# Modulation rows summed and turned by two picking matmuls per chunk, and the decay projection as fp32r products in the key stage

## The chip, the core and the metric

The kernel runs on one core of one Trainium2 chip. The metric is the device time of one execution in microseconds; the median of three runs before the change is 1827.17 us (1825.25 to 1828.84). Engines are named as in the profile: PE is TensorE, PEld its weight loads, DVE is VectorE, ACT is ScalarE, POOL is GpSimd, SP is the queue that issues most transfers. A line such as L281 is a line of the kernel before.

## The reference

One layer of a hybrid backbone on 256 latent tokens and 256 context tokens, 2048 wide. Both streams are first modulated by rows that come from a condition vector each, then projected by one matrix `w_in`:

```
sh_m, sc_m, ... = split(silu(c) @ w_ada + b_ada, 6)       # csh_m, csc_m from c_ctx
h_lat = x * (1 + sc_m) + sh_m;   h_ctx = ctx * (1 + csc_m) + csh_m
q, k, v, g, a_lr, p, bg = split(h @ w_in)                  # a_lr: 2 x 16 columns
z[d] = a_lr[:, 16d:16d+16] @ w_decay_up[d] + b_decay_up[d]  # d: forward, backward
log_decay[d] = log_sigmoid(z[d]) / 16
```

Keys, queries, values and decays go into a gated linear attention in both directions (4 heads, chunks of 64); latent scans start from the context's final state. A pooling branch runs beside it, both are gated, projected and normalised, and a SwiGLU network follows. All inputs are fp32.

## The kernel before

Weights arrive as 512 KB units of 128 x 1024 fp32 (`raw`) and are split into two fp32r parts, `hi` on ACT (L96) and `lo` on DVE (L97). A product is three matmuls on such parts (L155, L156, L158 where tokens are stationary; L125 and L129 where weights are). The modulated inputs are kept split in the same way, 16 slices of 128 channels, in the tiles `hl` (latent) and `hc` (context).

The first stage makes the inputs and the values `v` together, since modulation is needed slice by slice. `ada_chunk` makes the modulation of 1, 2 or 4 slices at a time: seven chunks, (0,1) (1,1) (2,2) (4,2) (6,2) (8,4) (12,4) as first slice and number n. For a chunk it

- sums `silu(cond) @ w_ada` in 16·n/4 units of 512 KB (`rw`, ten buffers); each unit is four plain fp32 matmuls with a 2-column stationary operand (c and c_ctx), one on each of four 32-column strips of the array, so that the sums lie in partitions 0-1, 32-33, 64-65, 96-97 of one PSUM bank (L281);
- copies or adds these strips into a row tile `rb` of 2 partitions, one operation per strip (L241, L243, L292);
- turns each 128 columns of the rows into a column, 2n small fp32 matmuls against a 2 x 2 identity (L295), and adds biases (L301);
- scales and shifts the input slices (`rx`, L307), adds their share of the decay projection `a_lr` to a PSUM bank `a_acc` by fp32 matmuls with a 32-column operand, one per slice and stream (L312), and splits them into `hl` and `hc`.

Four value blocks follow for every group of slices (L341 on); after each unit of value weights the generator `step` issues some of the next chunk's sums. Plain fp32 matmuls take two passes, so each counts as two instructions in the profile.

At the end of the values `a_acc` is copied, spread onto the partitions that the heads read by a selection table `selt` and a row of ones (L377, L378, two fp32 matmuls for each direction), and kept as `alr[d]`: parts hi, lo, hi of the rows at partitions 0, 32, 64, and bias rows. Then the PSUM pool of this stage is closed and one with four and four banks opened, and the key stage begins (`kT_half`, L125 and L129). `log_sigmoid` (L438) later multiplies `alr[d]` by `wd`, the decay weights of one head.

The order on each engine is made by a list scheduler that follows data, buffers and priorities; SP issues transfers in the order of that schedule and waits where a buffer is not free yet. A pool can wait for the whole pool whose place it takes, or tile by tile (`reuse_waits="tile"`).

## Time and profile before

| what | value |
|---|---|
| runs, median (lowest, highest) | 1827.17 us (1825.25, 1828.84) |
| profiled execution: time, span | 1823.62 us, 1821.7 us |
| granted clock, mean | 0.992 |
| busy: PE, DVE, ACT, POOL | 97%, 64%, 44%, 1% of the span |
| bytes read from HBM | 390.62 MB, 216 GB/s over the span |
| values stage | first matmul at 4.8 us, last value product at 261.3 us |
| key stage | first product at 267.15 us |
| head stage, first use of `alr` | 380.2 us |

A row of groups reads: line, engine, operation, output<-input by the program's names, shape, xcount | busy us, mean ns of one | idle time of the engine just before. A row of the timeline reads: start us, length us, engine, line, operation; x2 is two merged instructions, and brackets give an idle stretch before it with what ended it. Starts of matmuls are measured and their ends are modelled, so spacings of starts are the safer reading.

### The profile page before, as it was taken

What the parts mean: (1) busy time and instruction counts of PE and PEld (TensorE: products, weight loads), DVE (VectorE), ACT (ScalarE), POOL (GpSimd) and SP (SyncE); (2) the same over time, 40 slices, a digit from 0 to 9 for tenths busy, and PEclk for the clock granted to TensorE, in tenths of its full rate; (3) what the DMA queues carried; (4) which work ended last, traced back from release to release, by engine and by line L of the source; (5) the groups of instructions that cost most, each with busy time, mean ns of one, the idle gap of its engine ahead of it and who ended that gap; (6) DMA issues with size and microseconds to landing.
All of it is one profiled execution on the core that took longest, in us unless ns stands there. A gap on an engine that the chain in (4) does not pass through costs nothing.

```text
span 1821.7 us, 24845 instructions
## 1 busy us (share of the span) xinstructions
PE 1773.5 (97%) x9596; PEld 1466.1 (80%) x9596; DVE 1167.8 (64%) x1740; ACT 804.3 (44%) x1182; POOL 9.6 (1%) x20
## 2 busy tenths in 40 slices
PE   6999999999999999999999989999999999999996
PEld 3666778878777788888888878888888888888886
DVE  3555457578768888865656665678865556554555
ACT  2212222256666554454444454454444444433332
POOL 0000000000000000000000000000000000000000
PEclk9999999999999999999999989999999999999998
DMA  8696238576535688865557635579976555555553
GB/s 336 227 338 233 82 128 300 193 249 225 168 110 184 220 304 317 291 210 191 190 193 276 204 112 187 192 249 314 329 267 197 187 193 186 182 192 193 196 187 125
DMA packets 109702, 394.35 MB, mean 216 GB/s; under 512 B 12224, under 2 KB 12864, under 8 KB 109072
## 3 DMA queue, kind: packets, MB, share of 16 engines
q1 hardware_dynamic: 107712, 384.05, 61.6%
q0 software_dynamic: 1872, 8.72, 1.3%
q8 instruction: 75, 1.23, 0.3%
q14 instruction: 43, 0.35, 0.1%
HBM read 390.62 MB, written 2.10 MB: 216 GB/s over the span
## 4 chain that ended last, share of the span: by engine, by line
PE 64%; DMA 4%; DVE 3%; ACT 2%; issue 1%; SPq 0%; DVEq 0%; ACTq 0%
PE ps L125 28%; PE ps L129 14%; PE ps L158 6%; PE ps L155 6%; PE ps L156 6%; DMA raw<-in_w_o 1%; DMA ra<-in_w_adaT 1%; DVE lo L97 1%; ACT hi L96 1%; DMA raw<-in_w_fi 0%; DVE ra L267 0%; PE ps L110 0%; PE ps L494 0%; PE ps L112 0%; PE ps L111 0%
## 5 line engine op out<-in xcount | busy, mean ns | idle before, releaser
L97 DVE TENSOR_TENSOR lo<-raw,hi 128x1024 fp32r<-128x1024 f32 x510 | 622.2, 1222 | 415.3 <-ACT hi L96 401.0
L96 ACT ACTIVATE hi<-raw 128x1024 fp32r<-128x1024 f32 x510 | 539.0, 1059 | 671.2 <-PE ps L156 225.8
L125 PE MATMUL ps<-h,hi 128*128 128x512 f32 x1408 | 355.5, 394 | 3.4 <-ACT hi L96 2.6
L125 PEld LDWEIGHTS ps<-h,hi 128*128 128x128 f32 x1408 | 254.5, 190 | 49.7 <-ACT hi L96 2.8
L125 PE MATMUL ps<-hl,hi 128*128 128x512 f32 x768 | 212.2, 394 | 1.5 <-DVE alr L380 1.4
L129 PEld LDWEIGHTS ps<-h,lo 128*128 128x128 f32 x1408 | 192.5, 190 | 14.2 <-DVE lo L97 0.4
L129 PE MATMUL ps<-h,lo 128*128 128x256 f32 x1408 | 196.9, 282 | 0.0
L125 PEld LDWEIGHTS ps<-hl,hi 128*128 128x128 f32 x768 | 139.9, 189 | 27.9 <-DVE alr L380 2.2
L267 DVE SCALAR_TENSOR_TENSOR ra<-ra,silb 128x1024 f32<-128x1024 f32 x96 | 116.9, 1220 | 40.7 <-DMA ra<-in_w_adaT 40.2
L155 PE MATMUL ps<-hi,hid 128*128 128x512 f32 (+1 forms) x372 | 134.9, 369 | 0.0
L156 PE MATMUL ps<-hi,hid 128*128 128x512 f32 (+1 forms) x372 | 134.0, 369 | 0.0
L155 PE MATMUL ps<-hi,hl 128*128 128x512 f32 x320 | 129.7, 407 | 0.4 <-ACT hi L96 0.4
L156 PE MATMUL ps<-hi,hl 128*128 128x512 f32 x320 | 126.3, 396 | 0.0
L129 PE MATMUL ps<-hl,lo 128*128 128x256 f32 x768 | 120.7, 282 | 0.4 <-DVE lo L97 0.4
L129 PEld LDWEIGHTS ps<-hl,lo 128*128 128x128 f32 x768 | 111.5, 190 | 7.9 <-DVE lo L97 1.2
L158 PE MATMUL ps<-lo,hl 128*128 128x512 f32 x320 | 95.0, 394 | 0.0
L338 DVE TENSOR_TENSOR v<-ps,v 128x512 f32<-128x512 f32 x80 | 50.8, 683 | 62.3 <-PE ps L158 62.3
L158 PE MATMUL ps<-lo,hid 128*128 128x512 f32 x372 | 90.6, 369 | 0.0
L155 PEld LDWEIGHTS ps<-hi,hid 128*128 128x128 f32 x372 | 69.8, 188 | 12.2 <-DVE xt L749 0.2
L156 PEld LDWEIGHTS ps<-hi,hid 128*128 128x128 f32 x372 | 70.0, 188 | 11.9
L155 PEld LDWEIGHTS ps<-hi,hl 128*128 128x128 f32 x320 | 60.7, 190 | 21.8 <-issue 7.5
L158 PEld LDWEIGHTS ps<-lo,hid 128*128 128x128 f32 x372 | 66.2, 188 | 11.8
(244 smaller groups left out, 2111.9 us busy)
## 6 DMA issues: line engine op xcount, KB each, us to landing
raw<-in_w_fi SPq DMA_DIRECT2D x176, 512.0 KB, 3.4
ra<-in_w_adaT SPq DMA_DIRECT2D x96, 512.0 KB, 4.6
raw<-in_w_fo SPq DMA_DIRECT2D x88, 512.0 KB, 3.3
rw<-in_w_sh_sc SPq DMA_DIRECT2D x64, 512.0 KB, 7.5
raw<-in_w_bg SPq DMA_DIRECT2D x64, 512.0 KB, 3.8
raw<-in_w_v SPq DMA_DIRECT2D x32, 512.0 KB, 5.6
raw<-in_w_g SPq DMA_DIRECT2D x32, 512.0 KB, 4.2
raw<-in_w_go SPq DMA_DIRECT2D x32, 512.0 KB, 3.7
```

The lines of the kernel that those rows point to most:

```text
L96: S.activation(hi, full, AF.Copy)
L97: return V.tensor_tensor(lo, full, hi.bitcast(F32), op=ALU.subtract)
L125: PE.matmul(o, hi[:, j * P:(j + 1) * P], act(n + j), start=(n + j == 0), stop=(n + j == nk - 1), skip_group_check=True)
L129: PE.matmul(o[:, :T], lo[:, j * P:(j + 1) * P], act(n + j)[:, :T], start=False, stop=(n + j == nk - 1), skip_group_check=True)
L155: PE.matmul(o, ah, hi[:, a:b], start=(n + j == k0), stop=False)
L156: PE.matmul(o, al, hi[:, a:b], start=False, stop=False)
L158: PE.matmul(o, ah, lo[:, a:b], start=False, stop=(n + j == end))
L267: V.scalar_tensor_tensor(r, r, 1.0, silb[half], op0=ALU.mult, op1=ALU.mult, accum_out=mods[:, half, i:i + 1])
L338: V.tensor_tensor(dst, src, dst, op=ALU.add)
```

## The change

The stationary operand of the sums, `sil`, becomes 32 columns wide, 30 of them zero, so that a strip's 32 partitions are all written. One operation then copies the whole bank to `rb` (128 x 256, on DVE and ACT in turn), and two matmuls for each chunk, whose moving operand `pick` holds ones at the strips' rows, add the strips and turn them at once. Picks for n = 1 and 2 stand in new columns of the small table; n = 4 reads the identity.

The products of L312, `a_acc`, `selt` with its transfer, and the spread behind the values are gone. `decay_rows`, called once behind the first key tile, splits `w_a` into fp32r parts that stand side by side and multiplies them by the split inputs, 16 products for each stream; four ACT and five DVE operations add the parts and lay them out as one `alr` for both directions, whose weights `wdec` are zero where the other direction's rows stand. The transfer of `w_a` moves with it, from ahead of the first inputs on SP's queue to among the last value weights. PSUM pools wait tile by tile, and `a_acc`'s bank serves as a third bank for sums and picks.

```diff
@@ psum_pool, bank
-        return tc.tile_pool(name=name, bufs=1, space=bass.MemoryType.PSUM)
+        return tc.tile_pool(name=name, bufs=1, space=bass.MemoryType.PSUM, reuse_waits="tile")
...
-        return pool.tile([P, 512], F32, tag=kind, bufs=n if kind == "d" else (2 if n == 5 else 8 - n), name=nm("ps"))
+        return pool.tile([P, 512], F32, tag=kind, bufs=n if kind == "d" else 8 - n, name=nm("ps"))
@@ ada_chunk
-                    PE.matmul(pr[32 * g:32 * g + 2, :256], sil[:, kt, :], r[:, 256 * g:256 * g + 256],
+                    PE.matmul(pr[32 * g:32 * g + 32, :256], sil[:, kt, :], r[:, 256 * g:256 * g + 256],
...
-            if ci == 0:
-                nc.sync.dma_start(wa, w_a)
-            rb = pa.tile([P, U], F32, tag="rb", bufs=1, name=nm("rb"))
-            for g in range(4):
-                c = (g % n) * 256
-                if g < n:
-                    evac(rb[0:2, c:c + 256], pr[32 * g:32 * g + 2, :256], g % 2)
-                else:
-                    V.tensor_tensor(rb[0:2, c:c + 256], pr[32 * g:32 * g + 2, :256], rb[0:2, c:c + 256], op=ALU.add)
+            rb = pa.tile([P, T], F32, tag="rb", bufs=2, name=nm("rb"))
+            evac(rb, pr[:, :256], ci % 2)
             pc = bank("g")
-            for j in range(2 * n):
-                PE.matmul(pc[:, 2 * j:2 * j + 2], rb[0:2, P * j:P * j + P], ident[0:2, 0:2],
-                          start=(j == 0), stop=True, skip_group_check=True)
+            pcv = pc[:, :4 * n].rearrange("p (b j c) -> p b j c", j=2, c=2)
+            if n == 4:
+                pick = ident.rearrange("p (g r) -> p g r", r=32)[:, :, 0:2]
+            else:
+                c0 = S_S1 if n == 1 else S_S2
+                pick = sm[:, c0:c0 + 2 * n].rearrange("p (g c) -> p g c", c=2)
+            for j in range(2):
+                PE.matmul(pcv[:, :, j, :], rb[:, P * j:P * j + P], pick, start=(j == 0), stop=True, skip_group_check=True)
...
-                for j in range(n):
-                    kt = a + j
-                    g = kt % 4
-                    PE.matmul(a_acc[32 * g:32 * g + 32, si * T:(si + 1) * T], wa[:, kt, :], r[:, j * T:(j + 1) * T],
-                              start=(kt < 4 and si == 0), stop=(kt >= 12), skip_group_check=True)
@@ before the values
+        sil = pa.tile([P, KT, 32], F32, tag="sil", name="sil")
+        V.memset(sil, 0.0)
+        first = S.activation(sil[:, :, 0:2], sm[:, S_CT:S_CT + 32].rearrange("p (k c) -> p k c", c=2), AF.Silu)
@@ behind the values
-        nc.gpsimd.dma_start(selt, sel)
-        ones_r = pa.tile([1, 2 * T], F32, tag="rb", name="ones_r")
-        V.memset(ones_r, 1.0)
-        acc = pa.tile([P, 2 * T], F32, tag="rx", bufs=2, name="acc")
-        S.activation(acc, a_acc, AF.Copy)
-        for d in range(2):
-            o = bank("g")
-            PE.matmul(o, selt[:, d, :], acc, start=True, stop=False)
-            PE.matmul(o, selt[0:1, 2, :], ones_r, start=False, stop=True)
-            S.activation(alr[d], o, AF.Copy)
-            V.tensor_tensor(alr[d][32:64, :], o[32:64, :], alr[d][32:64, :].bitcast(F32), op=ALU.subtract)
@@ new, called behind the first key tile
+        def decay_rows():
+            wr = pq.tile([P, KT, 32], F32, tag="war", name="war")
+            nc.sync.dma_start(wr, w_a)
+            w2 = pq.tile([P, KT * 64 + 64], F32R, tag="wa", name="wa")
+            V.memset(w2[:, KT * 64:].bitcast(F32), 0.0)
+            w2v = w2[:, :KT * 64].rearrange("p (k s n) -> p k s n", s=2, n=32)
+            split(wr, w2v[:, :, 0, :], w2v[:, :, 1, :])
+            ones = pq.tile([P, 2 * T], F32, tag="aro", name="ones")
+            V.memset(ones, 1.0)
+            S.activation(alr[96:128, :], ones[96:128, :], AF.Copy)
...
+            for si, act in enumerate((lat_m, ctx_m)):
+                o = bank("g")
+                for kt in range(KT):
+                    PE.matmul(o, w2[:, 64 * kt:64 * kt + P], act(kt), start=(kt == 0), stop=(kt == KT - 1))
+                S.activation(t0[32:64, si, :], o[32:64, :], AF.Copy)
+                V.tensor_tensor(t0[0:32, si, :], o[0:32, :], t0[32:64, si, :], op=ALU.add)
+                V.tensor_tensor(full[0:32, si * T:(si + 1) * T], t0[0:32, si, :T], t0[0:32, si, T:], op=ALU.add)
+            S.activation(alr[0:32, :], full[0:32, :], AF.Copy)
+            S.activation(alr[64:96, :], full[0:32, :], AF.Copy)
+            V.tensor_tensor(alr[32:64, :], full[0:32, :], alr[0:32, :].bitcast(F32), op=ALU.subtract)
```

Three places show how the order moves. A row names the line, the operation, output<-input and the output's shape; the lines of the changed kernel stand three higher for the products (L158, L159, L161 for L155, L156, L158) and two lower for the sums (L279). On PE, where chunk (8,4) is finished in the midst of a value block, before:

```order
L295 MATMUL ps_1025<-sm,rb_1020 128x2 x2
L155 MATMUL ps_1074<-hi_1078,hc_82 128x512
L156 MATMUL ps_1074<-hi_1078,hc_82 128x512
L295 MATMUL ps_1025<-sm,rb_1020 128x2 x2
L155 MATMUL ps_1075<-hi_1078,hc_82 128x512
L295 MATMUL ps_1025<-sm,rb_1020 128x2 x2
L281 MATMUL ps_1061<-rw_1062,sil 2x256 x4
L156 MATMUL ps_1075<-hi_1078,hc_82 128x512
L158 MATMUL ps_1072<-lo_1079,hl_80 128x512
L312 MATMUL a_acc<-rx_1037,wa 32x256 x2
L158 MATMUL ps_1073<-lo_1079,hl_80 128x512
L312 MATMUL a_acc<-rx_1037,wa 32x256
```

and now:

```order
L279 MATMUL ps_730<-rw_967,sil 32x256 x4
L279 MATMUL ps_730<-rw_973,sil 32x256 x4
L293 MATMUL ps_981<-sm,rb_979 128x4x2 x2
L279 MATMUL ps_1003<-rw_1004,sil 32x256 x4
L158 MATMUL ps_1014<-hi_1020,hl_77 128x512
L159 MATMUL ps_1014<-hi_1020,hl_77 128x512
```

The turns stood one by one between value products and are now one pair between sums; the decay products that followed are gone. Over the whole values stage 18 groups of decay products and 12 groups of turns stood between value products from the end of chunk 2 on.

On PE at the end of the values, before:

```order
L158 MATMUL ps_1795<-lo_1830,hc_83 128x512
L158 MATMUL ps_1796<-lo_1830,hc_83 128x512
L377 MATMUL ps_1866<-acc,selt 128x512
L378 MATMUL ps_1866<-ones_r,selt 128x512
L377 MATMUL ps_1871<-acc,selt 128x512
L378 MATMUL ps_1871<-ones_r,selt 128x512
L125 MATMUL ps_1889<-hl_80,hi_1893 128x512
```

and now (L128 and L132 are the key products):

```order
L161 MATMUL ps_1719<-lo_1755,hl_78 128x512
L161 MATMUL ps_1720<-lo_1755,hc_80 128x512
L161 MATMUL ps_1721<-lo_1755,hc_80 128x512
L128 MATMUL ps_1799<-hl_77,hi_1803 128x512
L128 MATMUL ps_1800<-hc_79,hi_1803 128x512
```

The keys follow the values directly. The decay products now stand behind the first key tile:

```order
L132 MATMUL ps_1800<-hc_80,lo_1842 128x256
L390 MATMUL ps_1892<-hl_77,wa 128x512 x8
L390 MATMUL ps_1892<-hl_78,wa 128x512 x8
L390 MATMUL ps_1912<-hc_79,wa 128x512 x8
L390 MATMUL ps_1912<-hc_80,wa 128x512 x8
L128 MATMUL ps_1950<-hl_77,hi_1954 128x512
```

All 32 stand in one run, with nothing between them. On ACT at the start, before:

```order
L96 ACTIVATE hi_153<-raw_151 128x1024
L96 ACTIVATE hl_80<-rx_135 128x256
L96 ACTIVATE hc_82<-rx_141 128x256
L96 ACTIVATE hi_240<-raw_238 128x1024
L96 ACTIVATE hl_80<-rx_193 128x256
```

and now:

```order
L99 ACTIVATE hl_77<-rx_128 128x256
L99 ACTIVATE hc_79<-rx_133 128x256
L99 ACTIVATE hi_144<-raw_142 128x1024
L241 ACTIVATE rb_173<-ps_148 128x256
L99 ACTIVATE hl_77<-rx_181 128x256
```

The first value weights' hi copy stood ahead of the first input splits and now stands behind them.

More of the change, by code (lines that the diff above doesn't have):

```diff
@@ L225, in trunk @@
         p1 = c1.enter_context(tc.tile_pool(name="p1", bufs=1))
-        alr = [p1.tile([P, 2 * T], F32R, tag=f"alr{d}", name=f"alr{d}") for d in range(2)]
-        silb_c = []
+        alr = p1.tile([P, 2 * T], F32R, tag="alr", name="alr")
         def slv(name, dt=F32):
@@ L400, in kT_half @@
                 fold(kTc[b][:, i, :], outs[1])
+                if b == 0 and i == 0:
+                    decay_rows()
                 ada(ADA[2])
```

47 lines of the change are left out of this document (22 added, 25 removed).

## The prediction

> **What bounds the kernel now.** I read the page first, then the busy time by windows, the groups of one window, and the timeline of TensorE around the edited lines.
>
> ```profile
> span 1821.7 us, 24845 instructions
> PE 1773.5 (97%) x9596; PEld 1466.1 (80%) x9596; DVE 1167.8 (64%) x1740; ACT 804.3 (44%) x1182; POOL 9.6 (1%) x20
> ```
>
> TensorE is busy for 97% of the span. A busy TensorE is not one at its peak, so I cut the first 380 us at the places that the change touches.
>
> ```profile
> 0.00:27.50 27.50, 13.69 (x87) 4.62 (x87) 8.08 (x23) 6.68 (x10) 1.40 (x6) 0.98 0.91 339
> 27.50:61.20 33.70, 32.21 (x195) 20.71 (x195) 13.51 (x24) 8.85 (x14) 0.00 (x0) 0.92 0.71 272
> 61.20:194.30 133.10, 133.10 (x836) 85.16 (x836) 71.79 (x121) 26.85 (x32) 0.00 (x0) 1.00 0.68 253
> 194.30:261.60 67.30, 67.30 (x295) 54.59 (x295) 32.97 (x40) 17.61 (x18) 0.00 (x0) 1.00 0.29 94
> 261.60:267.20 5.60, 4.20 (x10) 1.09 (x8) 4.48 (x7) 1.19 (x2) 0.00 (x0) 1.00 0.44 162
> 267.20:272.10 4.90, 4.90 (x15) 3.86 (x16) 2.98 (x5) 0.00 (x0) 0.00 (x0) 0.65 0.87 316
> 272.10:380.00 107.90, 107.90 (x625) 95.42 (x624) 68.61 (x103) 30.74 (x44) 1.26 (x2) 1.00 0.74 247
> ```
>
> Columns: length, busy time of PE, PEld, DVE, ACT, POOL, granted clock, DMA share, GB/s. Call them A (start), B, C, D (rest of the values), E (handover), F (its echo) and K (keys). D holds nothing but 512-wide products: 67.3/295 = 0.228 us each. K is as dense. In C the same engine is never idle, yet it does other things too:
>
> ```profile
> L281 PE MATMUL ps<-rw,sil 128*2 128x256 f32 x358 | 22.5, 379 | 0.0
> L312 PE MATMUL a_acc<-rx,wa 128*32 128x256 f32 x51 | 11.6, 391 | 0.0
> L295 PE MATMUL ps<-sm,rb 2*128 2x2 f32 x48 | 7.2, 251 | 0.0
> ```
>
> So C has 836 - 358 - 51 - 48 = 379 products (86.4 us) and 46.7 us of modulation sums (L281), decay products (L312) and turns (L295). What one interruption costs, the timeline tells:
>
> ```profile
> 117.30 0.61 PE L158 MATMUL ps<-lo,hc 128*128 128x512 f32 x2
> 117.84 1.91 PE L281 MATMUL ps<-rw,sil 128*2 128x256 f32 x32
> 119.68 0.50 PE L155 MATMUL ps<-hi,hl 128*128 128x512 f32 x1
> ...
> 186.87 0.50 PE L158 MATMUL ps<-lo,hc 128*128 128x512 f32 x1
> 187.30 0.62 PE L312 MATMUL a_acc<-rx,wa 128*32 128x256 f32 x2
> 187.85 0.49 PE L158 MATMUL ps<-lo,hc 128*128 128x512 f32 x1
> ...
> 137.65 0.40 PE L156 MATMUL ps<-hi,hl 128*128 128x512 f32 x1
> 137.98 0.60 PE L295 MATMUL ps<-sm,rb 2*128 2x2 f32 x4
> 138.51 0.50 PE L155 MATMUL ps<-hi,hc 128*128 128x512 f32 x1
> 138.84 0.40 PE L156 MATMUL ps<-hi,hc 128*128 128x512 f32 x1
> ```
>
> A unit of sums is eight instructions, two rounds on four strips: (1.91 - 0.38)/7 = 0.22 a round, 0.44 a unit. Going in and out adds 119.68 - 117.30 - 2 x 0.228 - 4 x 0.44 = 0.2, and 0.1 more in the first product behind (138.84 - 138.51 = 0.33, here behind a turn). One decay group costs 187.85 - 186.87 - 0.228 = 0.75, though its two instructions stream 0.43; one group of turns costs (1.19 - 0.456) = 0.73. By this price list C is 86.4 + 44.75 units x 0.44 + 17 groups of sums x 0.3 + 18 decay groups x 0.75 + 12 turns at 0.73 (0.2 less for the three that adjoin sums) = 132.9 of 133.1; the group counts are those of TensorE's order. The sum closes, so these prices may be used.
>
> **The change, part by part.** *C, decay products.* All 18 groups go: 13.5 us; at least their 11.6 us of busy time. *C, turns.* Twelve groups of four become four of four (two matmuls of two passes for each of four chunks). A pick that uses all rows is in no row of this trace; I bound a group by 0.25 and 0.73, take 0.5, near the latter because the four weight loads stay 128 wide: 8.2 - 2.0 = 6.2. Together C loses **19.7** (bounds 15 and 21.7). DVE's fewer partial sums lie beside this.
>
> *A, start.* The chain is: fourth transfer, sums, copy and adds, turn, scale, split, product.
>
> ```profile
> 11.49 1.03 PE L281 MATMUL ps<-rw,sil 128*2 128x256 f32 x8 [0.22 <-DMA rw<-in_w_sh_sc]
> 13.04 1.33 DVE L292 TENSOR_TENSOR rb<-ps,rb 2x256 f32<-2x256 f32 x3
> 16.50 0.42 ACT L96 ACTIVATE hc<-rx 128x256 fp32r<-128x256 f32 x1
> 18.05 1.22 PE L155 MATMUL ps<-hi,hl 128*128 128x512 f32 x2
> 22.12 1.04 PE L281 MATMUL ps<-rw,sil 128*2 128x256 f32 x16
> 25.15 0.57 PE L295 MATMUL ps<-sm,rb 2*128 2x2 f32 x4 [1.99 <-DVE rb L292]
> 27.48 0.80 PE L155 MATMUL ps<-hi,hl 128*128 128x512 f32 x1
> ```
>
> The 192 KB table ahead of the fourth transfer goes (0.6 us at A's 339 GB/s) and the adds (1.33): the split of hc ends at 16.92 - 1.9 = 15.0. But on ACT the weight's hi copy now stands behind hc, 1.06 us as elsewhere: first product near 16.2 instead of 18.05. From there to the last sums of chunk 1 it took 4.07 with eight products and two units; now eight and one, 3.6. From those sums to 27.48 it took 5.36; now one unit more (+0.44), no adds (-1.33), no decay pair between (-0.5, between 0 and 0.75): 16.2 + 3.6 + 4.0 = 23.8. The sil operand now waits for a DVE memset, and ACT's table load sits behind the small table's transfer; both are hidden while they end before 11.49, when the fourth transfer is there. A loses **3.7**: at least the 1.85 of the first product, at most 6.2, if only the data's landing set it.
>
> *B.* 195 instructions are 88 products (20.1), 90 of sums (11.25 units, 4.9), 8 turns, 9 decay. With four groups at 0.3 this makes 26.2 of 33.7; 7.5 are decay, turns, a slow clock (0.92) and this wait:
>
> ```profile
> 57.57 1.02 PE L295 MATMUL ps<-sm,rb 2*128 2x2 f32 x8 [1.49 <-DVE rb L292]
> ```
>
> Chunk 2 is needed at once, so its chain stays exposed: copy 0.6, picks 0.5, scale and split about 1.1, plus 1.5 of slow clock near the new start. That is 3.7 of the 7.5, and one group fewer: **4.1** (1 to 6.5).
>
> *E and F, handover.*
>
> ```profile
> 261.12 0.61 PE L158 MATMUL ps<-lo,hc 128*128 128x512 f32 x2
> 263.43 1.28 DVE L338 TENSOR_TENSOR v<-ps,v 128x512 f32<-128x512 f32 x2
> 267.15 0.50 PE L125 MATMUL ps<-hl,hi 128*128 128x512 f32 x1 [1.41 <-DVE alr L380]
> 268.75 0.63 PE L125 MATMUL ps<-hl,hi 128*128 128x512 f32 x1
> 271.31 0.63 PE L125 MATMUL ps<-hl,hi 128*128 128x512 f32 x1
> ```
>
> The last value product ends its stream at 261.6, the first key product starts at 267.15: 5.6 us for the spread of the decay rows. Then the clock falls: products come 0.43 apart from 268.75 to 271.31, and F's 15 take 4.9 instead of 3.4. Both go, 7.1; keys may still wait for a bank to be emptied, 0.5 taken: **6.5** (4 at the least, by the third rival).
>
> *K.* 32 products of 512 columns are added in one run: 32 x 0.228 = **7.3**. Their weights are fetched and split during D: 256 KB on SP's queue, moved from ahead of the first inputs to among the last value weights, where the DMA share is 0.29 and DVE is busy 32.97 of 67.3; the split is one ACT and one DVE operation of half a weight's size. The fan-out (five DVE and four ACT operations of at most 0.68) has cover: DVE works 68.6 of K's 107.9, and nothing needs alr before the heads. I add 0.3; without cover, 4.1.
>
> Sum: -19.7 - 3.7 - 4.1 - 6.5 + 7.3 + 0.3 = **-26.4**. Everything behind keeps its work and its order up to single rows, on an engine that is full there. The profiled execution took 1823.62, 3.6 below the median of the runs shown, 1827.17; I carry the difference over: 1797.2 in the profile, **1800.8** as a median.
>
> **Rivals.** *Wide weights show.* The sums now load 32 columns where they loaded 2:
>
> ```profile
> L281 PEld LDWEIGHTS ps<-rw,sil x512: 80/84/86, 4.8 to 176.4; 128*2 128x2 f32 x171
> L312 PEld LDWEIGHTS a_acc<-rx,wa x64: 106/109/173, 16.2 to 193.5; 128*32 128x32 f32 x64
> 59.81 0.38 PE L312 MATMUL a_acc<-rx,wa 128*32 128x256 f32 x1
> 60.02 0.38 PE L312 MATMUL a_acc<-rx,wa 128*32 128x256 f32 x1
> 145.04 0.63 PE L312 MATMUL a_acc<-rx,wa 128*32 128x256 f32 x6
> ```
>
> A load takes 25 ns more. If all 512 showed it, 12.8 us are lost: 1813.6. Against it: with 32-wide loads two instructions follow at 0.21, the same round. The Trainium skill ("TensorE: Matmul & The Clock Gate", "What overlaps and what doesn't") says that a load overlaps running matmuls only if their row groups differ; these all use the same rows, so by it the loads would show. The trace speaks against that. 10%.
>
> *The strips no longer run side by side,* the slower side: with wide weights a unit would take eight rounds, 1.76 instead of 0.44; 64 x 1.32 = 84 lost, 1885. It is slower than before once a unit exceeds 0.44 + 26.4/64 = 0.85. Against it stands the row at 145.04: six 32-wide instructions in three strips take 0.63, as two do at 187.30. 3%.
>
> *The banks hold the keys back.* The last V drain ends at 264.71, 3.1 us after the last product. If keys need those banks, 2.6 more is lost and the slow clock (1.5) returns: 1804.9. The changed pools wait bank by bank, and four of the eight banks hold no values by then; 10%. The same page's "The two states you'll see" wants an idle window of about 3.4 us before the clock halves; here no idle stretch in E exceeds 1.41 us and it fell all the same, so I leave the 1.5 in.
>
> *The transfers become the bound.* C moves the same bytes in 113 us: a DMA share of 0.68 becomes 0.80, while A held 0.91. If bursts capped it at 0.75, C would end 7.3 later: 1808. 6%.
>
> *More is won,* if data alone set the start and B: 1794. 7%.
>
> **How the numbers follow.** The forecast holds 62%, with its own range 1795 to 1808; 2% is left for anything unnamed. The bounds together allow 1793 to 1816. The range 1793 to 1814 takes in the wide loads and the banks. A change of 0.2% (3.7 us) is what a measurement of this kernel can tell. All cases but the strips and the unnamed are faster, 95%; since a spread of small waits could hide here I give 0.92 faster, 0.03 same, 0.05 slower.
>
> **What would show it.** Right: in the changed profile a unit of sums keeps rounds of 0.22; value products stand alone between sums; the first key product starts near 235, at full clock; one run of 32 products of 7.3 us follows behind the first key tile; K is otherwise as dense. Wrong: gaps before sums that transfers end, rounds above 0.22, or keys waiting for DVE.

## The result, and the profile after

The changed kernel takes 1811.97 us (1810.72 to 1814.48), the kernel before, run beside it, 1826.72: a ratio of 0.992 with a 95% interval of 0.9903 to 0.9937, so 14.75 us faster. The forecast was 1800.8, that is 26.4 us faster. The profiled executions are 12.9 us apart (1823.62 and 1810.72), and the working below is made against these. The page of the changed kernel begins:

```profile
span 1808.9 us, 24699 instructions
PE 1754.6 (97%) x9520; PEld 1469.2 (81%) x9520; DVE 1163.7 (64%) x1729; ACT 804.3 (44%) x1181; POOL 9.1 (1%) x19
```

TensorE is as full as before, so what was won and lost has to be sought by place. The changed kernel's busy time by windows, cut at the ends of the start, of chunk (2,2), of the last chunk and of the values (columns as in the prediction):

```profile
0.00:26.00 26.00, 12.25 (x81) 5.52 (x81) 5.14 (x17) 5.37 (x9) 0.87 (x5) 1.00 0.91 333
26.00:54.80 28.80, 28.25 (x191) 19.84 (x191) 13.99 (x23) 10.30 (x16) 0.00 (x0) 1.00 0.84 324
54.80:172.00 117.20, 113.49 (x749) 82.58 (x747) 67.92 (x112) 23.40 (x27) 0.00 (x0) 0.99 0.77 290
172.00:239.20 67.20, 67.20 (x294) 54.51 (x293) 36.51 (x48) 19.69 (x20) 0.54 (x1) 1.00 0.37 124
```

The kernel before had no idle TensorE in C (133.10 of 133.10). The third window now has 3.7 us of it. The two longest of TensorE's waits up to the end of the values:

```profile
PE ps L279 <- DMA rw<-in_w_sh_sc: 8.8, 2, 5.4
PE ps L158 <- ACT hi L99: 5.7, 2, 3.2
```

The columns are the total, the number of waits and the longest. The first row is the start, as before. The second is new: twice a value product waits for the hi copy of its weights on ScalarE. One is at the start, the other of 3.2 us near 120 us.

To see how the gain runs through the program I took the start times of matching events in both traces. The gain is the time before less the time after.

| event | before | changed | gain |
|---|---|---|---|
| first product of slice group (2,2), behind A and B | 61.20 | 53.55 | 7.7 |
| drain of the 19th of 24 value blocks, behind C | 206.03 | 183.68 | 22.3 |
| first key product | 267.15 | 239.22 | 27.9 |
| after the slow clock of F | 270.89 | 241.71 | 29.2 |
| first product behind the run of 32 | 280.00 | 257.61 | 22.4 |
| first use of `alr` | 380.28 | 357.86 | 22.4 |
| a fixed product in the gates | 899.03 | 880.81 | 18.2 |
| first product of the FFN's output | 1565.59 | 1552.89 | 12.7 |

So 29 us are won in the first 242 us, 7 are spent on the new products, and then the gain shrinks once more, from 22.4 to 12.7, in code that the change leaves alone but for the layout of the decay rows. From the FFN's output to the end both take 256 us.

### The profile page after: what moved, and what is told of

Same layout as the page of the kernel before. It is cut to its first block, busy times and chain, and to the rows that moved or that the text cites. A ratio compares the mean times of both kernels' runs of the same rounds, so it can differ in the third digit from the quotient of the medians.

```text
span 1808.9 us, 24699 instructions
## 1 busy us (share of the span) xinstructions
PE 1754.6 (97%) x9520; PEld 1469.2 (81%) x9520; DVE 1163.7 (64%) x1729; ACT 804.3 (44%) x1181; POOL 9.1 (1%) x19
## 3 DMA queue, kind: packets, MB, share of 16 engines
q0 software_dynamic: 1808, 8.52, 1.3%
q8 instruction: 74, 1.21, 0.3%
## 4 chain that ended last, share of the span: by engine, by line
PE 80%; DMA 10%; DVE 6%; issue 2%; ACT 2%; SPq 0%; DVEq 0%; ACTq 0%
PE ps L128 28%; PE ps L132 14%; PE ps L158 11%; PE ps L159 10%; PE ps L161 10%; DMA ra<-in_w_adaT 5%; DVE lo L100 2%; PE ps L279 2%; DMA fa<-in_w_adaT 1%; DMA raw<-in_w_o 1%; ACT hi L99 1%; PE ps L504 1%; PE ps L547 1%; DMA raw<-in_w_fi 1%; DVE ra L265 1%
## 5 line engine op out<-in xcount | busy, mean ns | idle before, releaser
L128 PE MATMUL ps<-h,hi 128*128 128x512 f32 x1408 | 357.5, 396 | 4.5 <-ACT hi L99 3.7
L128 PEld LDWEIGHTS ps<-h,hi 128*128 128x128 f32 x1408 | 255.9, 191 | 51.4 <-ACT hi L99 4.1
L128 PE MATMUL ps<-hl,hi 128*128 128x512 f32 x768 | 211.1, 392 | 0.5 <-ACT hi L99 0.5
L132 PEld LDWEIGHTS ps<-h,lo 128*128 128x128 f32 x1408 | 193.1, 191 | 15.9 <-DVE lo L100 2.2
L132 PE MATMUL ps<-h,lo 128*128 128x256 f32 x1408 | 198.1, 283 | 0.4 <-DVE lo L100 0.4
L128 PEld LDWEIGHTS ps<-hl,hi 128*128 128x128 f32 x768 | 139.3, 189 | 25.9 <-ACT hi L99 0.7
L158 PE MATMUL ps<-hi,hl 128*128 128x512 f32 x320 | 128.9, 404 | 9.1 <-ACT hi L99 7.9
L158 PE MATMUL ps<-hi,hid 128*128 128x512 f32 (+1 forms) x372 | 134.9, 369 | 0.0
L159 PE MATMUL ps<-hi,hid 128*128 128x512 f32 (+1 forms) x372 | 134.0, 369 | 0.0
L159 PE MATMUL ps<-hi,hl 128*128 128x512 f32 x320 | 126.2, 396 | 0.0
L132 PE MATMUL ps<-hl,lo 128*128 128x256 f32 x768 | 120.5, 282 | 0.0
L132 PEld LDWEIGHTS ps<-hl,lo 128*128 128x128 f32 x768 | 111.7, 190 | 7.0 <-DVE lo L100 0.2
L161 PE MATMUL ps<-lo,hl 128*128 128x512 f32 x320 | 93.2, 392 | 0.0
L161 PE MATMUL ps<-lo,hid 128*128 128x512 f32 x372 | 90.6, 369 | 0.0
L158 PEld LDWEIGHTS ps<-hi,hl 128*128 128x128 f32 x320 | 60.4, 189 | 28.4 <-ACT hi L99 8.7
L158 PEld LDWEIGHTS ps<-hi,hid 128*128 128x128 f32 x372 | 69.9, 188 | 12.2 <-DVE xt L759 0.2
L159 PEld LDWEIGHTS ps<-hi,hid 128*128 128x128 f32 x372 | 70.0, 188 | 11.9
L161 PEld LDWEIGHTS ps<-lo,hid 128*128 128x128 f32 x372 | 66.2, 188 | 11.8
```

The lines of the kernel that those rows point to most:

```text
L128: PE.matmul(o, hi[:, j * P:(j + 1) * P], act(n + j), start=(n + j == 0), stop=(n + j == nk - 1), skip_group_check=True)
L132: PE.matmul(o[:, :T], lo[:, j * P:(j + 1) * P], act(n + j)[:, :T], start=False, stop=(n + j == nk - 1), skip_group_check=True)
L158: PE.matmul(o, ah, hi[:, a:b], start=(n + j == k0), stop=False)
L159: PE.matmul(o, al, hi[:, a:b], start=False, stop=False)
L161: PE.matmul(o, ah, lo[:, a:b], start=False, stop=(n + j == end))
```

## The experiments

Before the runs stood two theories. One: the values lost a part of the forecast gain to the order on ScalarE, where a weight's hi copy is queued behind an input split that waits for the sums. The other: the prices themselves were wrong (32-wide weights, picks, new products). For the loss behind the keys, the theory was crowded transfers. Since one stretch can be read to a few tenths in a trace and a whole execution cannot, many verdicts are taken from stretches.

### The two halves of the change, alone

The modulation half put into the kernel before:

```diff
-                    PE.matmul(pr[32 * g:32 * g + 2, :256], sil[:, kt, :], r[:, 256 * g:256 * g + 256],
+                    PE.matmul(pr[32 * g:32 * g + 32, :256], sil[:, kt, :], r[:, 256 * g:256 * g + 256],
...
-            rb = pa.tile([P, U], F32, tag="rb", bufs=1, name=nm("rb"))
-            for g in range(4):
...
-            for j in range(2 * n):
...
+            rb = pa.tile([P, T], F32, tag="rb", bufs=2, name=nm("rb"))
+            evac(rb, pr[:, :256], ci % 2)
...
+            for j in range(2):
+                PE.matmul(pcv[:, :, j, :], rb[:, P * j:P * j + P], pick, start=(j == 0), stop=True, skip_group_check=True)
```

> The kernel before with only the modulation part of the change: 32-wide weights, one copy of the sums and two picking matmuls per chunk; the decay accumulators, their 36 products and the selection at the end stay. By the prediction's prices the turn groups fall from 8.2 to about 2.0 us in the values and the copies of the first chunks shorten by 0.9 us each, so 6 to 9 us faster than the kernel before, about 1819 us. If the 32-wide weight loads show, 512 loads x 25 ns come on top: about 1832 us. If the picks gain nothing: 1827 us.

Measured: 1813.78 us (1809.00 to 1823.26), ratio 0.9939 (0.9909 to 0.997), by the ratio 11 us faster. At the 19th value block it is 13.7 us ahead, more than the 6 to 9 expected.

The decay half alone is the changed kernel with the old sums and turns:

```diff
-            rb = pa.tile([P, T], F32, tag="rb", bufs=2, name=nm("rb"))
-            evac(rb, pr[:, :256], ci % 2)
+            rb = pa.tile([P, U], F32, tag="rb", bufs=1, name=nm("rb"))
+            for g in range(4):
...
```

> The changed kernel with the old modulation sums: 2-wide weights, four copies or additions of the sums and 2n turns per chunk; the decay products run in the keys and the accumulators are gone. By the prediction's prices: values -13.5, start and second chunk about -3, handover -6.5, keys +7.3, so about 15 us faster than before, 1811 us. The trace of the changed kernel has a new 4.8 us wait near 118 us, where the value weights' hi copy queues on ScalarE behind the input split of the fifth chunk; here that copy is queued ahead of the chunk's copies, so no such wait is expected. If the two parts simply add and no new wait is to blame, then this gain and that of the modulation part alone add up to the 14.75 us of the whole change; if the queue is to blame they add up to some 20 us or more.

Measured: 1814.73 us (1809.99 to 1817.79), ratio 0.9929 (0.9901 to 0.9956), by the ratio 13 us faster. At the 19th block it is 15.0 ahead. The two halves alone make 13.7 + 15.0 = 28.6 there; the whole change makes 22.3. Not all of the 6.3 us between them is a loss of the combination. At the first product of group (2,2) the halves have 7.4 and 3.1, the whole 7.7, so 2.8 are missing there already, where both halves are compared with the same spell of slow clock: it lasts 6.83 us from 26.2 us in the kernel before, 3.41 us with the decay half alone, and does not occur in the other two. Only from the 12th block's drain to the 19th's (3.9 and 7.3 in the halves, 7.8 in the whole) are 3.4 us lost that the halves alone do not lose.

### The order on ScalarE

The chunk (8,4) is where the wait stands. TensorE in the changed kernel:

```profile
118.34 1.50 PE L279 MATMUL ps<-rw,sil 128*32 128x256 f32 x24
120.34 0.61 PE L293 MATMUL ps<-sm,rb 128*128 128x8 f32 x4 [0.50 <-ACT rb L241]
120.88 0.64 PE L279 MATMUL ps<-rw,sil 128*32 128x256 f32 x8
124.73 0.80 PE L158 MATMUL ps<-hi,hl 128*128 128x512 f32 x1 [3.21 <-ACT hi L99]
125.33 0.63 PE L159 MATMUL ps<-hi,hl 128*128 128x512 f32 x1
125.75 0.63 PE L158 MATMUL ps<-hi,hl 128*128 128x512 f32 x1
```

and ScalarE:

```profile
105.42 1.06 ACT L99 ACTIVATE hi<-raw 128x1024 fp32r<-128x1024 f32 x1 [5.17 <-DMA raw<-in_w_v]
119.91 0.38 ACT L241 ACTIVATE rb<-ps 128x256 f32<-128x256 f32 x1 [13.43 <-PE ps L279]
122.68 1.06 ACT L99 ACTIVATE hl<-rx 128x1024 fp32r<-128x1024 f32 x1 [2.39 <-DVE rx L304]
123.64 1.04 ACT L99 ACTIVATE hi<-raw 128x1024 fp32r<-128x1024 f32 x1
```

ScalarE stands idle for 13.43 us until the sums are done, copies them, stands idle again until VectorE has scaled the input, splits it, and only then copies the weights. The value products do not need that split; they need the weights. Behind the wait the products come 0.4 to 0.6 apart. The edit moves the copies of the sums to VectorE, after which the scheduler puts the weights' copy first:

```diff
-            evac(rb, pr[:, :256], ci % 2)
+            evac(rb, pr[:, :256], 0)
```

> The changed kernel with one edit: every copy of a chunk's sums runs on VectorE (before: odd chunks on ScalarE). In the order of ScalarE the value weights' hi copy then stands ahead of the fifth chunk's input split, which was behind it. Theory: the 4.8 us wait near 118 us and the 1.3 us of half clock behind it go, 5 to 6 us faster than the changed kernel, about 1806 us. Rival: the wait is the chunk's own chain (last sum, copy, picks, scaling), whatever the order on ScalarE; then 1812 us and the wait stays.

Measured: 1806.54 us (1805.58 to 1813.62), ratio 0.99 (0.987 to 0.993). The interval overlaps that of the changed kernel, so the time alone does not tell the two apart; the trace does. TensorE and ScalarE of this run:

```profile
119.92 0.61 PE L293 MATMUL ps<-sm,rb 128*128 128x8 f32 x4 [0.80 <-DVE rb L239]
120.46 0.64 PE L279 MATMUL ps<-rw,sil 128*32 128x256 f32 x8
121.03 0.50 PE L158 MATMUL ps<-hi,hl 128*128 128x512 f32 x1
121.36 0.40 PE L159 MATMUL ps<-hi,hl 128*128 128x512 f32 x1
```

```profile
114.49 1.06 ACT L99 ACTIVATE hi<-raw 128x1024 fp32r<-128x1024 f32 x1 [7.68 <-DMA raw<-in_w_v]
122.26 1.06 ACT L99 ACTIVATE hl<-rx 128x1024 fp32r<-128x1024 f32 x1 [6.71 <-DVE rx L304]
```

The weights are copied as they land, 6.5 us ahead of their use at 121.03, and the value products follow the sums directly at full clock. From the drain of the 12th block (110.24 in the changed kernel, 109.52 here) to that of the 19th (183.68 and 178.76) this kernel is 4.2 us shorter, and a spell of slow clock of 3.41 us behind the wait has gone with it. At the 19th block it is 27.3 us ahead of the kernel before, 4.9 more than the changed kernel (5 to 6 were expected). The theory holds for this place. What remains of the wait is 0.8 us for the sums' copy (0.5 in the changed kernel).

### Are the 32-wide weights free?

```diff
-                    PE.matmul(pr[32 * g:32 * g + 2, :256], sil[:, kt, :], r[:, 256 * g:256 * g + 256],
+                    PE.matmul(pr[32 * g:32 * g + 32, :256], sil[:, kt, :], r[:, 256 * g:256 * g + 256],
```

> The kernel before with nothing changed but the weights of the modulation sums, which are 32 columns wide (30 of them zeros) and write 32 rows; copies, turns and decay products stay. Theory: the four strips go on side by side and a 32-column load hides as a 2-column load does, so within 2 us of the kernel before, 1826 to 1829 us, and rounds of four stay at 0.22 us. Rival: 25 ns more for each of 512 loads, 12.8 us slower, 1839.5 us; if the strips go one after the other, tens of us slower.

Measured: 1828.55 us (1826.72 to 1836.60), ratio 1.0013 (0.9995 to 1.003). The rival's 12.8 us would be a ratio of 1.007 and lies outside. The loads in this kernel, and eight rounds of sums between value products:

```profile
L277 PEld LDWEIGHTS ps<-rw,sil x512: 106/110/177, 4.7 to 177.8; 128*32 128x32 f32 x171
119.01 1.93 PE L277 MATMUL ps<-rw,sil 128*32 128x256 f32 x32
```

Each load is 26 ns longer than before (84), and a round still takes (1.93 - 0.38)/7 = 0.22. This rules out the rival, and with it the serial strips.

### The handover

```diff
-        return tc.tile_pool(name=name, bufs=1, space=bass.MemoryType.PSUM, reuse_waits="tile")
+        return tc.tile_pool(name=name, bufs=1, space=bass.MemoryType.PSUM)
```

> The changed kernel with one word of the change undone: the pools of PSUM banks wait for each other as a whole again, not tile by tile; the decay accumulators stay away. Read in the span: first value product to first key product took 249.1 us before and 221.9 in the changed kernel. If the bank-by-bank release carries the handover, the keys' first product waits for the last copies of the values and the clock falls again: 3 to 6 us more, 225 to 228 us. If the removed accumulators and their selection alone carry it: 221.9 within 0.5.

Measured: the stretch takes 230.6, 8.8 more, and one execution 1824.48 us. By the 19th value block some 3.6 us of this had already gone (18.8 us ahead instead of 22.3), most of it in slow stretches of the clock between 17 and 30 us and from 126 to 133 us that have nothing to do with the edit: the two runs below in which only the selection table is put back are 18.8 and 19.6 us ahead at this block. The other 5 stand at the handover, and the slow clock behind it takes about 2 more:

```profile
242.40 0.61 PE L161 MATMUL ps<-lo,hc 128*128 128x512 f32 x2
247.64 0.77 PE L128 MATMUL ps<-hl,hi 128*128 128x512 f32 x1 [4.63 <-DVE v L330]
248.20 0.63 PE L128 MATMUL ps<-hc,hi 128*128 128x512 f32 x1
```

The changed kernel at the same place:

```profile
238.76 0.61 PE L161 MATMUL ps<-lo,hc 128*128 128x512 f32 x2
239.22 0.39 PE L128 MATMUL ps<-hl,hi 128*128 128x512 f32 x1
239.44 0.39 PE L128 MATMUL ps<-hc,hi 128*128 128x512 f32 x1
```

So without the bank-by-bank release the wait for the drains takes the place of the wait for the decay rows almost in full. The handover's gain needs this one keyword; taking the decay rows away without it moved little there (18.8 us ahead at the 19th block, 19.5 at the first key product, 19 behind the slow clock). The keyword alone, in the kernel before with its decay rows in place, was not run, so what it is worth by itself is not shown.

### The new products

```diff
-                for kt in range(KT):
-                    PE.matmul(o, w2[:, 64 * kt:64 * kt + P], act(kt), start=(kt == 0), stop=(kt == KT - 1))
+                for kt in range(1):
+                    PE.matmul(o, w2[:, 64 * kt:64 * kt + P], act(kt), start=True, stop=True)
```

> The changed kernel with 2 instead of 32 decay products in the keys (the first slice alone, so the decays are not the reference's; everything else runs). The prediction's price is 0.228 us a product: 30 fewer take 6.8 us from the stretch between the first key product and the first product of the heads (118.6 us in the changed kernel, 113.1 before), so 111.8 us, and all of it is kept to the end of the mixer. Rival: the products fill time in which TensorE waits anyway, the stretch stays within 1 us of 118.6.

Measured: 111.85 against 118.64, 6.8 us for 30 products. Nothing covers them. The fan-out behind them runs in both kernels, so this run does not price it. The one execution took 1808.38 us: the 6.8 do not show in full there, because this execution came to its first key product 3.5 us later than the changed kernel's, again for the most part in slow clock from 26.5 to 30 us and from 125.5 to 132 us, and lost 2 more between the heads and the gates.

### The start

On top of the copies on VectorE, the first weights' hi copy is put ahead of the first splits (the two helpers that pass its handle on are left out here):

```diff
+            if ci == 0:
+                copied = []
+                early.append(weights(w_v[0], copied))
             for si, (src, dst) in enumerate(((xT, hl), (ctxT, hc))):
...
+                with tc.issue_after(copied[0].ins) if ci == 0 else ExitStack():
                     split(r[:, :n * T].rearrange("p (k t) -> p k t", t=T), d[:, :, 0, :], d[:, :, 1, :])
```

> The changed kernel with the copies of the sums on VectorE and the hi copy of the very first value weights ordered ahead of the first chunk's splits on ScalarE (its load is issued ahead of the two input loads). Theory: in the changed kernel the first value product at 17.36 us waits only for that copy, which stands behind two splits; with it ahead the first product comes 0.4 us after the first split, near 16.2 us as the prediction had it, and the second chunk's first product about 1 us earlier than its 25.96. Rival: the loads set the start, the weights land too late to be copied earlier; 17.3 us.

Measured: the first value product starts at 15.26 us, that of the second chunk at 24.16, 2.1 and 1.8 earlier than in the changed kernel. ScalarE at the start of the changed kernel, and TensorE here:

```profile
15.95 0.41 ACT L99 ACTIVATE hc<-rx 128x256 fp32r<-128x256 f32 x1
16.27 1.04 ACT L99 ACTIVATE hi<-raw 128x1024 fp32r<-128x1024 f32 x1
```

```profile
13.03 1.02 PE L299 MATMUL ps<-sm,rb 128*128 128x2 f32 x4 [0.55 <-DVE rb L245]
15.26 1.22 PE L164 MATMUL ps<-hi,hl 128*128 128x512 f32 x2 [1.22 <-ACT hl L99]
```

It is the same fault as near 120 us. Against the run with the copies on VectorE, whose first product starts at 17.06, 1.0 is left at the 19th block (28.3 ahead instead of 27.3). The one execution took 1809.98 us in all, as the FFN was slower in it (below).

### Behind the keys: transfers

The next rows are from the crowded part of the FFN, where the last quarter of the adaLN weights is loaded beside the FFN's own. First the kernel before, then the changed one:

```profile
1340.00:1345.00 5.00, 2.69 (x16) 2.20 (x14) 0.63 (x1) 0.85 (x1) 0.00 (x0) 1.00 1.01 415
1345.00:1350.00 5.00, 4.74 (x24) 4.07 (x25) 4.73 (x7) 3.07 (x6) 0.00 (x0) 1.00 0.48 141
```

```profile
1322.00:1327.00 5.00, 4.90 (x30) 4.15 (x28) 1.49 (x3) 1.37 (x2) 0.00 (x0) 1.00 0.99 406
1327.00:1332.00 5.00, 2.23 (x5) 1.84 (x6) 2.21 (x4) 2.58 (x4) 0.00 (x0) 0.71 0.59 235
1332.00:1337.00 5.00, 5.00 (x19) 4.27 (x18) 3.57 (x5) 2.81 (x5) 0.00 (x0) 0.61 0.75 243
```

Both kernels stall on weights that land late while the DMA engines are full (share 0.99 to 1.01). Before, the stall is 2.6 us and the clock stays; in the changed kernel it is 2.9 us after smaller ones, and the clock falls, so that 19 products go through in the last 5 us where 29 do in the undisturbed kernels below (748 in 130 us). On every engine the order here is the same in both kernels. To take the crowding away, the products that consume these loads were tied to one FFN tile each, on top of the edits of "The order on ScalarE" and "The start":

```diff
-                V.scalar_tensor_tensor(r, r, 1.0, silf[half], op0=ALU.mult, op1=ALU.mult,
-                                       accum_out=mods[:, half, 48 + i:49 + i])
+                with tc.issue_after(lo_ins.ins):
+                    V.scalar_tensor_tensor(r, r, 1.0, silf[half], op0=ALU.mult, op1=ALU.mult,
+                                           accum_out=mods[:, half, 48 + i:49 + i])
```

> The kernel of the run before with one more edit far behind the change: in the FFN the 32 products for the last quarter of adaLN are tied to one FFN tile each, so that their 16 MB of loads do not run ahead in 150 us beside the FFN's weights. Theory: the 5.5 us by which the changed kernel's FFN is slower than the kernel's before, with the same order on every engine, come from stalls on late weights while the DMA engines are at 0.9 of their time (first FFN up to output products: 666.6 us before, 672.1 changed, counted from the middle of the gates); paced, no stall is left and this stretch falls to 662 us or less in this kernel, in all about 1797 us. Rival: the stretch is slower for another reason and stays at 671 to 672; 1805 us.

Measured: 1799.42 us (1796.74 to 1800.62), ratio 0.9846 (0.9823 to 0.9869). With its three edits this is the fastest version, 28 us faster than the kernel before and, by the two ratios, 0.7% faster than the change as it stands. The stretch is 665.3, not quite the 662 expected. The same edit in the kernel before:

> The kernel before with the one edit of the paced run: the 32 products of the last adaLN quarter are tied to one FFN tile each. In the paced form of the changed kernel the stretch from the middle of the gates to the first FFN output product was 665.3 us (unpaced 676.5 in the same call, 672.1 in the changed kernel's profile). If the 5.5 us between the two kernels there are only stalls on late loads in the crowded part of the FFN, this kernel paced comes to the same 665.3 within 1 us, 666.6 unpaced. If the changed kernel is slower there for another reason, it comes to about 660.

Measured: 663.8, 2.7 less than unpaced (666.6); one execution took 1821.24 us. The 130 us that end 200 us ahead of the FFN's first output product, in the kernel before, the changed one, and the paced forms of both:

```profile
1235.59:1365.59 130.00, 127.43 (x730) 111.68 (x729) 100.31 (x147) 63.13 (x94) 1.05 (x2) 1.00 0.86 302
```

```profile
1222.89:1352.89 130.00, 125.89 (x699) 108.99 (x699) 96.40 (x143) 60.15 (x90) 1.05 (x2) 0.97 0.83 291
```

```profile
1233.23:1363.23 130.00, 130.00 (x748) 114.50 (x747) 89.21 (x122) 63.45 (x95) 0.00 (x0) 1.00 0.74 244
```

```profile
1212.82:1342.82 130.00, 130.00 (x744) 114.34 (x743) 89.89 (x122) 63.39 (x94) 0.00 (x0) 1.00 0.75 247
```

Paced, neither kernel has an idle TensorE or a lowered clock here. The two stretches differ by 1.5 us instead of 5.5, more than the 1 us expected, but the rest stands outside the crowd: 1.0 us is one wait of the paced form at 1520 us for VectorE. From the product 1400 places ahead of the FFN's first output product to the one 1000 places ahead it takes 38.3 us in the kernel before, 43.6 in the changed one, and 35.4 in both paced forms. So the loss in the FFN is stalls in the crowd and the slow clock behind them.

Why the changed kernel is hit harder by the same order of loads is another question. The stretch is 664.7 to 667.9 us in the profiles of the kernel before, of the modulation half alone and of the 32-wide weights alone; it is 670.9 to 676.5 in the six unpaced kernels above that contain the decay half, with or without the lowered clock (in one of the six, that with 30 products less, it stays up). The selection table, which the decay half drops, lay among the inputs ahead of the FFN's weights and was loaded at the start on GpSimd's queue. Three kernels ask whether that is it. The table left among the inputs of the changed kernel:

```diff
-          w_sh_sc, w_v, w_q, w_k, w_a, w_g, w_p, w_bg, w_go, w_pg, w_po, w_adaT,
+          w_sh_sc, w_v, w_q, w_k, w_a, sel, w_g, w_p, w_bg, w_go, w_pg, w_po, w_adaT,
```

> The changed kernel with the selection table of before still in its old place among the inputs, though nothing reads it: the tensors behind it, the FFN's weights and w_adaT among them, lie in memory as before. The instructions and their order are those of the changed kernel. Read in the span: from the middle of the gates to the first FFN output product, 664.7 to 667.9 us in the three kernels with the table and 670.9 to 676.5 us in the six without it that do not pace the adaLN loads. If where the inputs lie sets it: 668 or less. If it is what the decay part does to the queues or buffers: 671 or more.

Measured: 672.7, and 1813.40 us. Where an input lies that nothing reads no trace shows, so this run alone would not settle it. The table moved to the end of the inputs of the kernel before:

```diff
-          w_sh_sc, w_v, w_q, w_k, w_a, sel, w_g, w_p, w_bg, w_go, w_pg, w_po, w_adaT,
-          w_o, w_fi, w_fo, out):
+          w_sh_sc, w_v, w_q, w_k, w_a, w_g, w_p, w_bg, w_go, w_pg, w_po, w_adaT,
+          w_o, w_fi, w_fo, sel, out):
```

> The kernel before with the selection table as the last input instead of in the middle: instructions and order are those of the kernel before, and the weights behind the table lie as in the changed kernel. If where the inputs lie sets the FFN's stretch: 671 us or more in place of 666.6, and the whole some 5 us slower than the kernel before. If it is the decay part: 664 to 668 as before.

Measured: 665.5, and 1822.63 us. The table loaded again in the changed kernel, into a tile that nothing reads:

```diff
+        selt = pa.tile([P, 3, P], F32, tag="sel", name="selt")
+        nc.gpsimd.dma_start(selt, sel)
```

> The changed kernel with the selection table back among the inputs and loaded at the start on GpSimd's queue as before, into a tile that nothing reads; every other engine's order is that of the changed kernel. The loads on GpSimd's queue then count as before, and the inputs lie as before. If one of these sets the FFN's stretch: 668 us or less. If not: 671 or more, and what the decay part does to that stretch stays open.

Measured: 672.6, and 1812.85 us. All three speak against the table. What makes this stretch slower with the decay half stays open.

## Why the prediction was right, and where its sum was not

The direction, the main mechanisms and the outer range were right: faster, inside 1793 to 1814. The size was not: 26.4 us forecast, 12.7 by the events above (14.75 between the medians). The forecast's own range, 1795 to 1808, was missed by 4 us. That 1811.97 still lies in the outer one is partly luck: its upper end was there for the wide loads and the banks, and neither came about; what came about has no price in the sum. By the prediction's own terms:

| term | forecast | measured | from |
|---|---|---|---|
| A and B, start and chunk (2,2) | -7.8 | -7.7 | to the first product of group (2,2) |
| C | -19.7 | -14.7 | from there to the 19th block |
| E and F, handover | -6.5 | -6.8 | 19th block to 241.7 us |
| K | +7.6 | +6.8 | to the first product behind the run of 32 |
| everything behind | 0 | +9.7 | 22.4 to 12.7 |

**A and B.** The sum is right, its parts are not. The first product came at 17.36 and the second chunk's at 25.96, not at 16.2 and 23.8. The step that failed is the fourth transfer: the sums of that unit started at 12.24 us, 0.75 later than before instead of 0.6 earlier, although the table ahead of them was gone:

```profile
12.24 0.20 PEld L279 LDWEIGHTS ps<-rw,sil 128*32 128x32 f32 x8 [1.00 <-DMA rw<-in_w_sh_sc]
```

The 1.06 for the hi copy behind hc was right, and with that copy ahead the first product came at 15.26. B made up for it: 7.7 less the 1.5 of A is some 6.2, near the upper bound of 1 to 6.5, where 4.1 was taken. That is luck in part. The kernel before lost time here to a slow clock from 26.2 to 33.0 us, and the profiled execution of the changed kernel did not. In four other runs that do the same work up to there (the pools as a whole, 30 products less, the table kept, the table loaded) the clock fell near 26 us as well, and A and B together gain 5.4 to 6.2 instead of 7.7.

**C.** The price list held, but not the bounds: 14.7 lies under the lower one. (By the prediction's own prices these would have been 16.9 and 20.7, not 15 and 21.7: 11.6 and 13.5 for the decay groups, 5.3 and 7.2 for the turns.) A round is 0.22, and decay and turn groups are gone. A pick group that stands alone adds 164.91 - 163.53 - 4 x 0.228 = 0.47, counted as the prediction counted a turn (0.5 taken):

```profile
163.53 0.62 PE L161 MATMUL ps<-lo,hl 128*128 128x512 f32 x2
163.99 0.51 PE L293 MATMUL ps<-sm,rb 128*128 128x8 f32 x4
164.35 0.72 PE L161 MATMUL ps<-lo,hl 128*128 128x512 f32 x2
164.91 0.40 PE L158 MATMUL ps<-hi,hl 128*128 128x512 f32 x1
```

Without the ScalarE wait C is 18.9 shorter (8.4 us ahead at the first product of group (2,2), 27.3 at the 19th block), against 19.7. The missing step is a wait: the prediction saw the hi copy move behind the splits at the start, priced it there, and did not ask where else the same order would arise. The order shown with the change even had the place where it does, chunk (8,4), but only TensorE's order was looked at there, not ScalarE's. Before, the turns of that chunk stood one by one between value products, so its chain had cover; as one pair between sums it has none, and what is queued behind it on ScalarE waits too.

**E and F.** Right, and for the reason named under the third rival: the pools wait bank by bank. The rival priced the other case at 4.1; it measured about 7.

**K.** Right. The run of 32 stands behind the first key tile at full clock, from 250.32 to the next product at 257.61, 7.3 us. The 0.3 for the fan-out is not seen, and 0.5 came back elsewhere in the stretch:

```profile
250.32 3.82 PE L390 MATMUL ps<-hl,wa 128*128 128x512 f32 x16
253.98 3.79 PE L390 MATMUL ps<-hc,wa 128*128 128x512 f32 x16
```

**Everything behind.** This is the largest miss: "Everything behind keeps its work and its order up to single rows, on an engine that is full there." Work and order were kept, but time was not. 5.5 us went in the crowded part of the FFN, as shown. The other 4.2 went between the first use of `alr` and the gates. There the traces only suggest a cause, and executions differ: this stretch takes 515.9 to 518.7 us in three runs with the order of the kernel before, and 521.5 to 523.0 in three with that of the changed one. The first gate product waits 2.19 us for weights that land late, where the kernel before waits 0.39 (TensorE, then ScalarE, of the changed kernel):

```profile
360.45 0.50 PE L158 MATMUL ps<-hi,hl 128*128 128x512 f32 x1 [2.19 <-ACT hi L99]
```

```profile
359.34 1.06 ACT L99 ACTIVATE hi<-raw 128x1024 fp32r<-128x1024 f32 x1 [5.41 <-DMA raw<-in_w_g]
```

And VectorE's products for the other adaLN weights wait longer for their loads than before (of the kernel before, then of the changed one; total and number of waits):

```profile
  DMA ra<-in_w_adaT: 40.2, 43
```

```profile
  DMA ra<-in_w_adaT: 71.6, 56
```

The same 96 loads now follow a shorter front. That it is this which costs the 4.2 was not tested by a run of its own; in the kernels with one half alone the same stretch is 0.2 and 1.9 longer than before.

**The rivals.** Wide weights and serial strips are refuted. "The transfers become the bound" was looked for in the wrong place: in C the DMA share rose from 0.68 to 0.77 and no sum waited for a transfer (the last column is TensorE's idle time ahead of them, from 54.8 to 172 us), but in the heads and the FFN, which the prediction left out, loads do end the waits.

```profile
L279 PE MATMUL ps<-rw,sil 128*32 128x256 f32 x355 | 22.7, 383 | 0.0
```

The Trainium skill ("TensorE: Matmul & The Clock Gate", "What overlaps and what doesn't") has a weight load overlap running matmuls only if the row groups differ; the run with 32-wide weights alone does not agree, since 512 longer loads on the same rows cost nothing that shows.

## What to carry to other kernels

An engine that works in order is part of every chain queued on it: when a step becomes a single block that waits, list what stands behind it on each engine it touches, not only on the one that the edit speeds up, and do so at every place where the step recurs. "Nothing changes behind" is a term of the sum like any other; where a later stage runs at a full transfer rate, give it a price of its own, since a stall can also lower the clock behind it. And when a drain and a computation both stand at a stage's end, removing one may show little unless the other has been given its own way out. Last, before a gain of a few microseconds is put down to an edit, look whether a spell of slow clock came or went with it.

## What was not expected of the hardware

The same stall in the FFN shows when the clock falls. Its length alone does not tell. Stalls of 2.46 (32-wide weights alone), 2.53 (30 products less), 2.62 (the kernel before) and 3.00 us (the table kept) left the products behind them 0.23 apart. (Lengths are spacings of starts, less the 0.228 of a product.) Stalls of 2.84, 2.91, 2.92, 2.92, 3.08 and 3.90 us, in six of the kernels with the decay half, were followed by products 0.43 apart, at once or a few products later.

The instants of the falls tell more; the traces record the granted clock. In the changed kernel's trace it falls at 124.20, 1042.38, 1329.10 and 1796.73 us; the distances are 269.0, 84.0 and 137.0 times 3.413 us. In the other traces, too, falls lie whole multiples of 3.41 us apart, and each spell of slow clock but the last, which runs to the end of the program, lasts 3.41, 6.83 or 10.24 us. So the clock seems to be decided once in 3.41 us, on a grid that starts elsewhere in each execution. The window ahead of the FFN's fall and the spell behind it, in the changed kernel, and the window that holds most of the stall with the table kept:

```profile
1325.69:1329.10 3.41, 1.21 (x10) 0.97 (x8) 0.00 (x0) 0.43 (x1) 0.00 (x0) 1.00 1.00 413
1329.10:1335.93 6.83, 6.16 (x19) 5.22 (x20) 4.97 (x7) 4.72 (x8) 0.00 (x0) 0.50 0.55 194
```

```profile
1330.79:1334.20 3.41, 1.55 (x11) 1.26 (x9) 0.00 (x0) 0.02 (x1) 0.00 (x0) 1.00 1.01 414
```

TensorE is idle for 3.41 - 1.21 = 2.20 of the first window and for 3.41 - 1.55 = 1.86 of the last; the rest of the 3.00 us fell into the window behind. Over these ten stalls the split is clean: the clock fell where 2.15 us or more of the stall lay in one window, and stayed where it was 1.86 or less. The Trainium skill ("TensorE: Matmul & The Clock Gate", "The two states you'll see") gives an idle window of about 3.4 us that runs freely. The length and the free running agree with these traces; that the whole window has to be idle does not, since 2.15 us of 3.41 were enough. The grid was read from the traces afterwards, and no run was made to move a stall against it.

A lowered clock cost the changed kernel about as much as the stall that brought it: 19 products in the 5 us behind it, where 29 is the rule. Executions of kernels that are the same up to there also differ by up to 3.6 us at the first key product (239.2 in the changed kernel, 242.8 with the table kept), most of it in such spells. The wait near 120 us, the same 3.2 us in both, is followed by one of 3.41 us in the changed kernel and by one of 6.83 us with the table kept.
